# Gated networks with the first products by 2x2 blocks in seven block products, gated values through DRAM, second products by chunk

## The chip, the cores and the metric

One core of a Trainium2 chip runs the whole program. TensorE (PE) multiplies, VectorE (DVE), ScalarE (ACT) and GpSimd (POOL) do the rest, and SyncE (SP) issues most of the DMAs, each of its instructions in order. The metric is the device time of one execution in microseconds (us).

## The reference, cut to what matters

Two layers; each is a token mixer (layer 0: a state space model, S5, with a gated output; layer 1: attention with 8 heads) and a SwiGLU network. There are 1024 latent and 256 context tokens, 1024 features, and 2816 inner features.

```
def swiglu(h, w_in, w_out):
    gate, up = jnp.split(h @ w_in, 2, axis=-1)
    return (jax.nn.silu(gate) * up) @ w_out
...
    val, gate = jnp.split(z @ w_glu, 2, axis=-1)
    return (val * jax.nn.sigmoid(gate)) @ w_out, jnp.stack(finals, axis=1)
...
  x <- LayerNorm(alpha * x + gate * sublayer(x * (1 + scale) + shift)).
```

## The kernel before, in words

Activations lie feature-major: 8 k-tiles of 128 features by three chunks of tokens (CH): chunk 0 and chunk 1 with 512 latent tokens each, chunk 2 with the 256 of the context. They live in 88 "pages" (128 x 512 floats) and 13 half pages. Every product is made of three passes in fp32r: each operand is split into hi (ACT copies it, L95 and L124) and lo (DVE subtracts, L96 and L125), and `mm3` (L110) multiplies hi by hi (L114), hi by lo (L116) and lo by hi (L118), with n matmuls each for the chunks that it is given.

Weights are blocks of 128 x 1024, used in the order of `wseq`. `w_load` starts their loads on SP into two raw tiles (`wr`), `w_ahead` splits them by halves up to LS blocks ahead of the one that `w_next` hands out.

There are three gated networks: the mixer's output of layer 0 (8 tiles of 128 inner features, 8 outer ones) and two SwiGLU networks (22 tiles). In each, `glu_head` makes the first tile or two by chunk, `glu_body` (L717) the rest: for each inner tile one weight block of the gate and one of the value, each over all three chunks at once (`gemm_all`); `glu_gate` (L680) takes the activation on ACT (L685), multiplies by the value on DVE (L688) and splits the result. After every two inner tiles `out_all` multiplies them by their two blocks of the second weights, and DVE adds the scaled sums to the residual `acc` in SBUF (L655, `accumulate`). The last six tiles' second products are left for `tail_units`, by chunk, with their weights split once and kept.

`boundary` (L879) puts the end of a network, its layer norm and the next first products together: the products of chunk 0, then those of chunk 1 with the steps of chunk 0's norm between them, then those of chunk 2 with chunk 1's norm, then the next network's first tiles (heads) by chunk. An estimated clock and the list YW set after how many us of products the next step of a norm is emitted. The norm (`layer_norm`, L803) has matmuls of its own in PE's stream: the mean (L818), the mean square (L834), and the spread of the inverse root (L814), and on DVE the subtraction (L821), the sum of squares (L825, L829), the scaling (L844) and half of the affine maps (L849); POOL makes the lo of h (L852).

## Time and profile before

| | |
|---|---|
| median of 3 runs | 3405.5 us (3402.41 to 3406.01) |
| span of the profiled execution | 3407.8 us |
| PE busy | 3308.8 us, 18298 matmuls |
| DVE, ACT, POOL busy | 1781.3, 1071.3 and 368.6 us |
| bytes moved by DMA | 244.99 MB |

The profiled execution's own time is its span, from the first to the last instruction; the runs were timed apart from it, and their median is 2.3 us less than the span. A busy PE is not a PE at its peak: matmuls overlap, so that the pitch of their starts tells more than their durations. The rows further down name a line, an engine, an operation, the tile that it writes <- the tiles that it reads, shapes and counts.

### The profile page before, as it was taken

How to read it: one execution, taken by the hardware profiler on the slowest of the kernel's cores; microseconds unless marked ns; L12 is line 12 of the kernel's file. 1: busy time of each engine (PE TensorE's matmuls, PEld its weight loads, DVE VectorE, ACT ScalarE, POOL GpSimd, SP SyncE). 2: the span in 40 equal slices, each digit the busy share in tenths (PEclk: the TensorE clock that was granted, in tenths of full speed). 3: DMA queues.
4: the chain of work that ended last, by engine and by line, in shares of the span. 5: the costliest groups of instructions: out<-in, count | busy, mean ns of one | idle time of the engine just before them, and what ended most of it. 6: DMA issues, size and time to landing. Idle time of an engine off the chain costs nothing.

```text
span 3407.8 us, 45779 instructions
## 1 busy us (share of the span) xinstructions
PE 3308.8 (97%) x18298; PEld 2772.1 (81%) x18298; DVE 1781.3 (52%) x3883; ACT 1071.3 (31%) x2143; POOL 368.6 (11%) x387
## 2 busy tenths in 40 slices
PE   8999689999999999999999999999999999999997
PEld 5763678888888888888888899998888888888886
DVE  7789733246333333332476888887743333333226
ACT  3351441124211111111254577774431111111213
POOL 1230100015000000000153310000410000000002
PEclk9999899999999999999999999999999999999998
DMA  7679971110111111111112100003011111111111
GB/s 256 174 211 325 248 212 38 50 50 15 48 38 38 38 38 38 38 38 49 57 63 86 62 21 17 29 7 118 26 38 38 38 38 38 38 38 38 46 42 62
DMA packets 156372, 244.99 MB, mean 72 GB/s; under 512 B 46480, under 2 KB 86064, under 8 KB 155392
## 3 DMA queue, kind: packets, MB, share of 16 engines
q1 hardware_dynamic: 148672, 217.12, 20.5%
q0 software_dynamic: 7488, 24.96, 2.4%
q8 instruction: 143, 2.34, 0.3%
q14 instruction: 69, 0.57, 0.1%
HBM read 205.86 MB, written 36.18 MB: 71 GB/s over the span
## 4 chain that ended last, share of the span: by engine, by line
PE 88%; DVE 8%; DMA 1%; ACT 1%; issue 1%; POOL 1%; SPq 0%; DVEq 0%; ACTq 0%; POOLq 0%
PE ps L114 24%; PE ps L116 24%; PE ps L118 24%; PE ps L1179 3%; DVE sw L530 2%; PE ps L1200 1%; PE ps L1198 1%; PE ps L1199 1%; PE ps L1137 1%; PE ps L1138 1%; PE ps L1139 1%; DVE X L536 1%; DVE sw L534 1%; PE ps L596 1%; DMA G<-dPF 1%
## 5 line engine op out<-in xcount | busy, mean ns | idle before, releaser
L114 PE MATMUL ps<-pg,pg 128*128 128x512 f32 (+1 forms) x3888 | 1103.6, 369 | 7.2 <-ACT pg L124 3.3
L116 PE MATMUL ps<-pg,pg 128*128 128x512 f32 (+1 forms) x3888 | 1096.6, 367 | 1.3 <-POOL pg L852 1.0
L118 PE MATMUL ps<-pg,pg 128*128 128x512 f32 (+1 forms) x3888 | 1094.7, 367 | 0.2 <-DVE pg L96 0.2
L114 PEld LDWEIGHTS ps<-pg,pg 128*128 128x128 f32 x3888 | 658.7, 189 | 128.6 <-issue 5.4
L116 PEld LDWEIGHTS ps<-pg,pg 128*128 128x128 f32 x3888 | 658.5, 189 | 117.9 <-POOL pg L852 1.2
L118 PEld LDWEIGHTS ps<-pg,pg 128*128 128x128 f32 x3888 | 658.1, 189 | 115.8 <-DVE pg L96 0.5
L96 DVE TENSOR_TENSOR pg<-wr,pg 128x512 fp32r<-128x512 f32 x384 | 250.0, 696 | 515.9 <-ACT pg L95 511.3
L655 DVE SCALAR_TENSOR_TENSOR pg<-ps,mods,pg 128x512 f32<-128x512 f32 (+1 forms) x560 | 342.7, 660 | 258.5 <-PE ps L118 256.0
L124 ACT ACTIVATE pg<-pg 128x512 fp32r<-128x512 f32 x142 | 88.9, 631 | 1005.5 <-DVE pg L688 987.9
L688 DVE TENSOR_TENSOR pg<-pg,ps 128x512 f32<-128x512 f32 x104 | 71.1, 683 | 528.3 <-PE ps L118 528.3
L95 ACT ACTIVATE pg<-wr 128x512 fp32r<-128x512 f32 x384 | 221.1, 628 | 213.7 <-PE ps L116 79.5
L642 POOL TENSOR_TENSOR pg<-pg,pg 128x512 f32<-128x512 f32 x8 | 10.4, 1297 | 2073.2 <-DVE pg L655 2073.2
L685 ACT ACTIVATE pg<-ps 128x512 f32<-128x512 f32 x104 | 57.0, 595 | 379.3 <-PE ps L118 379.3
L125 DVE TENSOR_TENSOR pg<-ps,pg 128x512 fp32r<-128x512 f32 (+1 forms) x210 | 141.9, 676 | 54.5 <-ACT pg L124 49.0
L1159 ACT ACTIVATE pg<-ps,nb,rq 128x512 f32<-128x512 f32 x192 | 148.8, 776 | 5.8 <-DVE sm L1168 2.6
L125 DVE TENSOR_TENSOR pg<-pg,pg 128x512 fp32r<-128x512 f32 x142 | 100.9, 716 | 84.4 <-ACT pg L124 84.1
L124 ACT ACTIVATE pg<-ps 128x512 fp32r<-128x512 f32 (+1 forms) x210 | 123.3, 587 | 55.2 <-PE ps L1179 47.7
L114 PE MATMUL ps<-hp,pg 128*128 128x256 f32 x480 | 138.0, 287 | 0.0
L1144 DVE TENSOR_REDUCE mx<-ps 128x1 f32<-128x512 f32 (+1 forms) x208 | 136.9, 660 | 1.3 <-PE ps L1139 1.3
L116 PE MATMUL ps<-hp,pg 128*128 128x256 f32 x480 | 136.4, 284 | 0.0
L118 PE MATMUL ps<-hp,pg 128*128 128x256 f32 x480 | 136.4, 284 | 0.0
L167 PE MATMUL ps<-gw,sS 128*32 128x512 f32 x384 | 114.4, 618 | 8.2 <-DMA gw<-in_w_mod 7.8
(314 smaller groups left out, 3877.2 us busy)
## 6 DMA issues: line engine op xcount, KB each, us to landing
gw<-in_w_mod SPq DMA_DIRECT2D x192, 256.0 KB, 5.2
wr<-in_w_ffn_in SPq DMA_DIRECT2D x88, 512.0 KB, 3.6
wr<-in_w_ffn_out SPq DMA_DIRECT2D x48, 512.0 KB, 3.5
dT<-to POOLq DMA_DIRECT2D x16, 512.0 KB, 4.4
U<-dUL SPq DMA_DIRECT2D x16, 512.0 KB, 4.9
wr<-in_w_s_glu SPq DMA_DIRECT2D x16, 512.0 KB, 3.7
x<-in_x SPq DMA_DIRECT2D x8, 640.0 KB, 8.7
wr<-in_w_s_out SPq DMA_DIRECT2D x10, 512.0 KB, 3.5
```

The lines of the kernel that those rows point to most:

```text
L95: nc.scalar.activation(hi, x, AF.Copy)
L96: nc.vector.tensor_tensor(lo, x, hi.bitcast(F32), op=ALU.subtract)
L114: mm(ps[c], wh, rh[c], start=first, stop=False)
L116: mm(ps[c], wh, rl[c], start=False, stop=False)
L118: mm(ps[c], wl, rh[c], start=False, stop=last)
L124: self.nc.scalar.activation(hi, src, AF.Copy)
L125: self.nc.vector.tensor_tensor(lo, src, hi.bitcast(F32), op=ALU.subtract)
L167: nc.tensor.matmul(g[32 * q:32 * q + 32, :], self.sS[:, k, :], t[k], start=(k < 4), stop=(k >= 4), tile_position=(0, 32 * q))
L655: self.nc.vector.scalar_tensor_tensor(acc[f][c], ps, gate[:, f, cd:cd + 1], acc[f][c], op0=ALU.mult, op1=ALU.add)
L1144: v.tensor_reduce(mx[:, kc:kc + 1], ps, axis=AX.X, op=ALU.max)
L1159: nc.scalar.activation(p, u["bank"].pop((qt, kc)), AF.Exp, bias=nb[:, 0:1], scale=rq, accum_out=sm[:, kc:kc + 1])
L1179: nc.tensor.transpose(pt[:, a, 128 * qt:128 * qt + 128], u["p"][qt, kt // 4][:, 128 * (kt % 4):128 * (kt % 4) + 128], self.ident)
```

## The change

Of each gated network, the first products of an inner tile over the 1024 latent tokens are seen as a product of 2x2 blocks: the weights by gate (A11, A12) and value (A21, A22) and by the first and last four k-tiles, the activations by the same k halves and by chunk (B11 is the first k half of chunk 0, B21 the last one, B22 the last k half of chunk 1). Seven block products with the sums S1 to S4 of weights and T1 to T4 of activations give what eight did. `ffn_pair` does one inner tile in nine steps (seven block products of 12 matmuls over 512 tokens, and two of 24 over the 256 context tokens); `i_step` makes the sums and splits of the weights, AHEAD = 4 items before they are used. The head tiles keep the plain form, and `x_sums` makes T1 to T4 beneath them.

The gated values go to DRAM (`spill`, tensor dI), and the second products are made afterwards, chunk by chunk over the whole depth (`out_chunks`): for each of 8 output features and each block of 8 k-tiles one weight block, loaded and split again for each chunk (`out_plan`), and the values read back and split once for each chunk (`z_ahead`). The residual goes to DRAM and comes back too (`keep`, `residual`). The attention's output product takes the same form. A third raw weight tile is added (`w_raw`), and the second weights are laid out by output feature.

```
+    def w_raw(self):
+        self.nr += 1
+        p = self.wpools[-(self.nr % 3 == 0 and len(self.wpools) == 2)]
+        return p.tile([P, 1024], F32, tag="wr", bufs=2 - (p is not self.wpools[0]), name=self.nm("wr"))
...
-            r = self.wpool.tile([P, 1024], F32, tag="wr", bufs=2, name=self.nm("wr"))
-            self.nc.sync.dma_start(r, self.wseq[self.wld])
+            r = self.w_raw()
+            n = self.wseq[self.wld].shape[1]
+            self.nc.sync.dma_start(r[:, :n], self.wseq[self.wld])
             self.wraw[self.wld] = r
...
+    def ffn_head(self, hh, hl, head, act, raw):
+        ls, self.LS = self.LS, 0
+        ws = [self.w_next() for _ in range(2 * head)]
+        self.LS = ls
+        s = {}
+        sums = []
+        def unit(t, half, c):
+            n = CH[c][1]
+            if c == 1 and t == half == 0:
+                self.x_start(hh, hl, raw)
+                sums.append(self.x_sums())
+                self.i_load()
+            ps = self.gemm(ws[2 * t + half], hh, hl, c)
+            if half == 0:
+                s[t, c] = self.pgn(n)
+                self.nc.scalar.activation(s[t, c], ps, act)
+            else:
+                x = s.pop((t, c))
+                self.nc.vector.tensor_tensor(x, x, ps, op=ALU.mult)
+                self.spill(t, c, x)
+            if sums:
+                for _ in range(16 // (4 * head)):
+                    next(sums[0], None)
+            if c == 2:
+                self.XC = [(hh[k][2], hl[k][2]) for k in range(KT)]
+                self.i_until(2 * t + half + 2)
+            return n / 100
+        return [[lambda t=t, h=h, c=c: unit(t, h, c) for t in range(head) for h in range(2)] for c in range(3)]
...
                 nc.gpsimd.tensor_tensor(hl[kt][c], t, hh[kt][c].bitcast(F32), op=ALU.subtract)
+                if raw is not None and c < 2:
+                    raw[kt][c] = t
...
+PROD = (("A11", "B11"), ("S1", "T1"), ("S2", "T2"), ("A12", "B21"), ("S3", "T3"), None, ("A22", "T4"), ("S4", "B22"), None)
+ITEMS = ("A11", "S1", "S2", "A12", "S3", "A22", "S4", "A21")
+NEED = (1, 2, 3, 4, 5, 5, 6, 7, 8)
+AHEAD = 4
...
+    def x_sums(self):
+        v, r = self.nc.vector, self.xr
+        for n in ("T1", "T2", "T3", "T4"):
+            for k in range(4):
+                t = self.page()
+                if n == "T1":
+                    v.tensor_tensor(t, r[k][1], r[k][0], op=ALU.subtract)
+                elif n == "T2":
+                    v.tensor_tensor(t, r[k + 4][1], self.xt["T1", k], op=ALU.subtract)
+                elif n == "T3":
+                    v.tensor_tensor(t, r[k + 4][1], r[k][1], op=ALU.subtract)
+                else:
+                    v.tensor_tensor(t, r[k + 4][0], self.xt["T2", k], op=ALU.subtract)
+                self.xt[n, k] = t
+                hi, lo = self.page(F32R), self.page(F32R)
+                self.nc.scalar.activation(hi, t, AF.Copy)
+                self.nc.gpsimd.tensor_tensor(lo, t, hi.bitcast(F32), op=ALU.subtract)
+                self.X[n].append((hi, lo))
+                yield
+        self.xr = self.xt = None
+    def i_load(self):
+        if self.il < len(self.pairs):
+            r = []
+            for h in range(2):
+                x = self.w_raw()
+                self.nc.sync.dma_start(x, self.win[2 * self.pairs[self.il] + h])
+                r.append(x)
+            self.iraw[self.il] = r
+            self.il += 1
+    def i_step(self):
+        nc = self.nc
+        v = nc.vector
+        n = 8 * len(self.pairs)
+        a, b, c = self.ik, self.ik - 1, self.ik - 2
+        self.ik += 1
+        if a < n:
+            i, name = a // 8, ITEMS[a % 8]
+            while self.il <= i:
+                self.i_load()
+            g, u = self.iraw[i]
+            A = {"A11": g[:, :512], "A12": g[:, 512:], "A21": u[:, :512], "A22": u[:, 512:]}
+            if name[0] == "A":
+                t = A[name]
+            else:
+                t = self.page()
+                x, y, op = {"S1": ("A21", "A22", ALU.add), "S2": ("S1", "A11", ALU.subtract),
+                            "S3": ("A11", "A21", ALU.subtract), "S4": ("A12", "S2", ALU.subtract)}[name]
+                x, y = (A[z] if z in A else self.isum[i, z] for z in (x, y))
+                v.tensor_tensor(t, x, y, op=op)
+            self.isum[i, name] = t
+        if 0 <= b < n:
+            i, name = b // 8, ITEMS[b % 8]
+            hi = self.ihi[i, name] = self.page(F32R)
+            nc.scalar.activation(hi, self.isum[i, name], AF.Copy)
+        if 0 <= c < n:
+            i, name = c // 8, ITEMS[c % 8]
+            hi, lo = self.ihi.pop((i, name)), self.page(F32R)
+            v.tensor_tensor(lo, self.isum[i, name], hi.bitcast(F32), op=ALU.subtract)
+            self.isp[i, name] = (hi, lo)
+            if name == "A21":
+                self.iraw.pop(i)
+                for z in ITEMS:
+                    self.isum.pop((i, z))
+                if self.il < i + 3:
+                    self.i_load()
+    def i_until(self, k):
+        while self.ik - 2 < min(k, 8 * len(self.pairs)):
+            self.i_step()
+    def spill(self, t, c, x):
+        o, n = CH[c]
+        self.nc.sync.dma_start(self.dI[t][:, o:o + n], x)
+    def ffn_last(self, s):
+        if s >= 4:
+            self.w_ahead(0.5 * (s - 3))
+    def ffn_pair(self, i, act, last=None):
+        nc = self.nc
+        v, mm = nc.vector, nc.tensor.matmul
+        t = self.pairs[i]
+        W = {}
+        e = {}
+        def product(ps, a, b, first, stop):
+            wh, wl = W[a]
+            for k in range(4):
+                xh, xl = self.X[b][k]
+                o = slice(P * k, P * k + P)
+                for j, (p, q) in enumerate(((wh, xh), (wh, xl), (wl, xh))):
+                    mm(ps, p[:, o], q, start=(first and k == 0 and j == 0), stop=(k == 3 and j == 2), skip_group_check=True)
+        def ctx(a, b):
+            ps = self.psum()[:, :256]
+            for k in range(KT):
+                wh, wl = W[(a, b)[k // 4]]
+                o = slice(P * (k % 4), P * (k % 4) + P)
+                xh, xl = self.XC[k]
+                for j, (p, q) in enumerate(((wh, xh), (wh, xl), (wl, xh))):
+                    mm(ps, p[:, o], q, start=(k == 0 and j == 0), stop=(k == KT - 1 and j == 2))
+            return ps
+        for s in range(9):
+            self.i_until(8 * i + NEED[s] + AHEAD)
+            if last:
+                last(s)
+            for z in ITEMS[:NEED[s]]:
+                if z not in W:
+                    W[z] = self.isp.pop((i, z))
+            if s == 0:
+                R = self.psum()
+                product(R, *PROD[s], True, True)
+                s1 = self.page()
+                nc.scalar.activation(s1, R, AF.Copy)
+            elif s == 1:
+                Q = self.psum()
+                product(Q, *PROD[s], True, True)
+            elif s == 2:
+                product(R, *PROD[s], False, True)
+                s2 = self.page()
+                nc.scalar.activation(s2, R, AF.Copy)
+            elif s == 3:
+                B = self.psum()
+                product(B, *PROD[s], True, True)
+                v.tensor_tensor(s1, s1, B, op=ALU.add)
+                nc.scalar.activation(s1, s1, act)
+            elif s == 4:
+                product(R, *PROD[s], False, True)
+                t22 = self.page()
+                v.tensor_copy(t22, Q)
+                v.tensor_tensor(t22, t22, R, op=ALU.add)
+            elif s == 5:
+                ps = ctx("A11", "A12")
+                g = self.half()
+                nc.scalar.activation(g, ps, act)
+            elif s == 6:
+                product(R, *PROD[s], False, True)
+                v.tensor_tensor(s1, s1, R, op=ALU.mult)
+                self.spill(t, 0, s1)
+            elif s == 7:
+                product(Q, *PROD[s], False, True)
+                v.tensor_tensor(s2, s2, Q, op=ALU.add)
+                nc.scalar.activation(s2, s2, act)
+                v.tensor_tensor(s2, s2, t22, op=ALU.mult)
+                self.spill(t, 1, s2)
+            else:
+                ps = ctx("A21", "A22")
+                v.tensor_tensor(g, g, ps, op=ALU.mult)
+                self.spill(t, 2, g)
+    def out_plan(self, wout, nk):
+        return [w[:, o:min(o + 1024, P * nk)] for _ in range(3) for w in wout for o in range(0, P * nk, 1024)]
+    def spilled(self, c, i):
+        o, n = CH[c]
+        z = self.pgn(n)
+        self.nc.sync.dma_start(z, self.dI[i][:, o:o + n])
+        return z
+    def residual(self, x, f, c):
+        o, n = CH[c]
+        self.nc.sync.dma_start(x, self.dX[f][:, o:o + n])
+    def z_ahead(self, k, load=None):
+        nk = self.znk
+        while self.zl < min(3 * nk, k + (ZL if load is None else load)):
+            self.zr[self.zl] = self.zraw(self.zl // nk, self.zl % nk)
+            self.zl += 1
+        while self.zk < min(3 * nk, k):
+            c = self.zk // nk
+            if c < 2:
+                hi, lo = self.page(F32R), self.page(F32R)
+            else:
+                p = self.page(F32R, (P, 2, 256))
+                hi, lo = p[:, 0, :], p[:, 1, :]
+            self.split(hi, lo, self.zr.pop(self.zk))
+            self.zs[c, self.zk % nk] = hi, lo
+            self.zk += 1
+    def out_chunks(self, acc, gate, residual):
+        v, g = self.nc.vector, self.nc.gpsimd
+        nk = self.znk
+        st = {}
+        def unit(c, f, lo):
+            o, n = CH[c]
+            hi = min(lo + 8, nk)
+            if lo == 0:
+                st["ps"] = self.psum()[:, :n]
+                acc[f][c] = self.pgn(n)
+                residual(acc[f][c], f, c)
+            w = self.w_next()
+            for i in range(lo, hi):
+                if f == 0:
+                    self.z_ahead(nk * c + i + 1 + ZS)
+                x, y = self.zs[c, i]
+                self.mm3([st["ps"]], *(z(P * (i - lo)) for z in w), [x], [y], i == 0, i == nk - 1)
+                if f == 7:
+                    self.zs.pop((c, i))
+                    if c < 2 and i >= 2:
+                        self.z_ahead(nk * (c + 1) + min(i - 1, ZE))
+            if hi == nk:
+                self.accumulate(acc, gate, f, c, st["ps"])
+                if f == 1:
+                    rs = self.rs[c] = self.pgn(n)
+                    g.tensor_tensor(rs, acc[0][c], acc[1][c], op=ALU.add)
+                if f > 1:
+                    (v if f == 7 else g).tensor_tensor(self.rs[c], self.rs[c], acc[f][c], op=ALU.add)
+            return 3 * (hi - lo) * n / 2220
+        return [[lambda c=c, f=f, o=o: unit(c, f, o) for f in range(8) for o in range(0, nk, 8)] for c in range(3)]
...
+ZL, ZS, ZE = 3, 2, 12
...
+        def keep(kt, c):
+            o, n = CH[c]
+            nc.sync.dma_start(self.dX[kt][:, o:o + n], acc[kt][c])
+        def body(act, nk, raw):
+            n = len(self.pairs)
+            for i in range(n):
+                self.ffn_pair(i, act, self.ffn_last if i == n - 1 else None)
+            self.X = self.XC = None
+            self.LS = 1.5
+            self.out_start(nk, raw)
...
+        def ffn(l, cols, outs, acc):
+            win = L("w_ffn_in", l)
+            self.wseq += win[:4]
+            self.i_start(win, range(2, NF))
+            raw = [[None] * 2 for _ in range(KT)]
+            self.cross(outs, acc, cols, lambda hh, hl: self.ffn_head(hh, hl, 2, AF.Silu, raw), keep, raw)
+            self.wseq += self.out_plan(L("w_ffn_out", l), NF)
+            body(AF.Silu, NF, self.spilled)
+            acc = new()
+            return self.out_chunks(acc, self.mod(l, 5), self.residual), acc
...
-        self.glu_body(zh, zl, *S5P, AF.Sigmoid, acc, self.mod(0, 2))
+        self.wseq += self.out_plan(L("w_s5_out"), KT)
         zh = zl = None
-        outs = self.glu_tail(8, 2, 4, acc, self.mod(0, 2))
...
+        body(AF.Sigmoid, KT, self.spilled)
...
-        self.wseq += self.glu_weights(L("w_ffn_in", 0), L("w_ffn_out", 0), *FFP)
-        hh, hl = self.cross(outs, acc, self.ln_cols(0, 0, 0, 3, 4), lambda hh, hl: self.glu_head(hh, hl, 2, AF.Silu))
-        self.glu_body(hh, hl, *FFP, AF.Silu, acc, self.mod(0, 5))
-        hh = hl = None
-        outs = self.glu_tail(NF, 2, 4, acc, self.mod(0, 5))
...
+        outs, acc = ffn(0, self.ln_cols(0, 0, 0, 3, 4), outs, acc)
...
+        self.wseq += self.out_plan(L("w_o"), KT)
+        self.LS = 1.5
+        self.out_start(KT, lambda c, h: self.ao[h][c])
+        ahead = {(k // 2, 2 * (k % 2)): [lambda k=k: self.w_ahead(0.5 * k + 0.5)] for k in range(3)}
+        ahead.update({(2 + k // 3, 2 * (k % 3)): [lambda k=k: self.z_ahead(k + 1, 0)] for k in range(6)})
+        ahead[4, 0] = [lambda: self.z_ahead(8, 0)]
...
-        self.out_all(ws.__getitem__, tl[0:2], acc, g, each=lambda: some(2))
-        ws = [self.w_next(), self.w_next()]
-        for i, j in enumerate((1, 3, 4, 6)):
-            todo.insert(j, lambda i=i: self.w_ahead(0.5 * i + 0.5))
-        self.out_all(ws.__getitem__, tl[2:4], acc, g, (0,), each=lambda: some(1))
-        some(len(todo))
-        self.LS = 2
-        self.ao = None
-        outs = self.tail_units(tl[4:] + tl[2:4], 4, acc, g)
...
+        outs = self.out_chunks(acc, self.mod(1, 2), self.residual)
+        outs, acc = ffn(1, self.ln_cols(1, 0, 1, 3, 4), outs, acc)
```

## Rows read from the trace of the kernel before

**Rows 1.** Span and mean granted clock of the core.

```profile
core 0: 3407.8 us, clock 0.984
```

**Rows 2.** The page's busy times: us, share, instructions of each engine.

```profile
PE 3308.8 (97%) x18298; PEld 2772.1 (81%) x18298; DVE 1781.3 (52%) x3883; ACT 1071.3 (31%) x2143; POOL 368.6 (11%) x387
```

**Rows 3.** The chain that ended last, shares by engine.

```profile
PE 88%; DVE 8%; DMA 1%; ACT 1%; issue 1%; POOL 1%; SPq 0%; DVEq 0%; ACTq 0%; POOLq 0%
```

**Rows 4.** Stretches: length, busy us (instructions) by engine, clock, DMA share, GB/s.

```profile
820.00:1680.00 860.00, 860.00 (x4398) 730.64 (x4397) 293.63 (x517) 151.88 (x289) 24.95 (x27) 1.00 0.13 41
740.00:820.00 80.00, 76.04 (x408) 65.17 (x407) 61.90 (x116) 33.77 (x53) 34.17 (x29) 0.98 0.09 27
1680.00:1760.00 80.00, 76.98 (x452) 67.12 (x451) 63.55 (x117) 34.02 (x52) 35.10 (x30) 0.98 0.14 47
2390.00:2460.00 70.00, 66.39 (x360) 57.54 (x359) 51.03 (x99) 29.14 (x43) 28.10 (x24) 0.95 0.08 26
3330.00:3408.00 78.00, 55.30 (x314) 47.96 (x312) 53.97 (x125) 27.34 (x45) 14.32 (x15) 0.84 0.19 68
```

**Rows 5.** Timeline of PE, three stretches: start, us, operation.

```profile
900.37 0.75 PE L116 MATMUL ps<-pg,pg 128*128 128x512 f32 x3
...
902.13 0.75 PE L116 MATMUL ps<-pg,pg 128*128 128x512 f32 x3
...
766.10 0.39 PE L118 MATMUL ps<-pg,pg 128*128 128x512 f32 x1
...
777.69 0.39 PE L118 MATMUL ps<-pg,pg 128*128 128x512 f32 x1
...
784.72 0.28 PE L118 MATMUL ps<-hp,pg 128*128 128x256 f32 x1
...
796.95 0.28 PE L118 MATMUL ps<-hp,pg 128*128 128x256 f32 x1
```

**Rows 6.** Groups by line and shape: count | busy us, mean ns | idle before.

```profile
L655 DVE SCALAR_TENSOR_TENSOR pg<-ps,mods,pg 128x512 f32<-128x512 f32 x384 | 272.0, 745 | 251.1 <-PE ps L118 248.6 <-DMA pg<-dX 2.3
L96 DVE TENSOR_TENSOR pg<-wr,pg 128x512 fp32r<-128x512 f32 x384 | 250.0, 696 | 515.9 <-ACT pg L95 511.3
L95 ACT ACTIVATE pg<-wr 128x512 fp32r<-128x512 f32 x384 | 221.1, 628 | 213.7 <-PE ps L116 79.5 <-DMA wr<-in_w_ffn_in 70.8 <-DMA wr<-in_w_o 30.5
L688 DVE TENSOR_TENSOR pg<-pg,ps 128x512 f32<-128x512 f32 x104 | 71.1, 683 | 528.3 <-PE ps L118 528.3
L852 POOL TENSOR_TENSOR pg<-pg,pg 128x512 fp32r<-128x512 f32 x48 | 64.6, 1378 | 50.1 <-ACT pg L851 50.1
L685 ACT ACTIVATE pg<-ps 128x512 f32<-128x512 f32 x104 | 57.0, 595 | 379.3 <-PE ps L118 379.3
L825 DVE TENSOR_TENSOR pg<-pg,pg 128x512 f32<-128x512 f32 x40 | 34.3, 857 | 0.0
L688 DVE TENSOR_TENSOR hp<-hp,ps 128x256 f32<-128x256 f32 x52 | 21.6, 415 | 7.0 <-PE ps L118 7.0
```

**Rows 7.** Timeline of DVE in a norm: start, us, operation.

```profile
1688.88 0.67 DVE L821 TENSOR_TENSOR pg<-pg,ps 128x512 f32<-128x512 f32 x1
1689.48 0.68 DVE L825 TENSOR_TENSOR pg<-pg,pg 128x512 f32<-128x512 f32 x1
```

**Rows 8.** DMA issues: count, KB each, median us from issue to landing.

```profile
wr<-in_w_ffn_in SPq DMA_DIRECT2D x88, 512.0 KB, 3.6
...
pg<-dQ SPq DMA_DIRECT2D x16, 256.0 KB, 2.8
```

**Rows 9.** Timeline of SP's queue: reload of the residual (14 of 256 KB, 7 of 128 KB).

```profile
2310.11 14.28 SPq L1386 DMA_DIRECT2D pg<-dX  x21
```

**Rows 10.** Timeline of PE about a stop in a norm.

```profile
758.05 1.06 PE L834 MATMUL ps<-ones,pg 128*128 128x1 f32 x8 [2.80 <-DVE pg L829]
...
759.55 0.63 PE L116 MATMUL ps<-pg,pg 128*128 128x512 f32 x1
759.97 0.63 PE L118 MATMUL ps<-pg,pg 128*128 128x512 f32 x1
```

**Rows 11.** What PE waited for: us in total, times, longest.

```profile
PE ps L834 <- DVE pg L829: 10.2, 4, 2.8
PE ps L834 <- DVE hp L829: 8.4, 2, 7.0
```

**Rows 12.** The chain that ended last, its end: start, us, what.

```profile
3382.90 0.49 DVE pg L655
...
3400.42 2.99 ACT pg L872 x5
```

More of the change, by code (lines that the diff above doesn't have):

```diff
@@ L800, in rsqrt, with layer_norm @@
             v.scalar_tensor_tensor(out if it == 2 else y, t, 1.5, y, op0=ALU.add, op1=ALU.mult)
-    def layer_norm(self, acc, c, cols, hh, hl, ready, after=None):
+    def layer_norm(self, acc, c, cols, hh, hl, ready, after=None, raw=None):
         nc = self.nc
@@ L1303, in run @@
             self.rest()
-            self.wpool.release()
+            for p in self.wpools[::-1]:
+                p.release()
             self.pages.release()
@@ L1313, in rest @@
         L = self.rows
-        S5P, FFP = self.S5P, (NF, 2, 2, 4)
+        new = lambda: [[None] * 3 for _ in range(KT)]
+        def keep(kt, c):
[18 more added lines that the diff above has]
+            return self.out_chunks(acc, self.mod(l, 5), self.residual), acc
+        self.wpools.append(tc.alloc_tile_pool(name="w2", bufs=1, side="left", reuse_waits="tile"))
         self.LS = 2
-        zh, zl = self.fm(F32R), self.fm(F32R)
-        zz = {}
+        zh, zl, zz = self.fm(F32R), self.fm(F32R), new()
         def zload(c):
@@ L1337, in rest @@
         zload(1)
-        heads = self.glu_head(zh, zl, 1, AF.Sigmoid)
+        self.i_start(L("w_s5_glu"), range(1, 8))
+        heads = self.ffn_head(zh, zl, 1, AF.Sigmoid, zz)
         zsplit(8)
@@ L1373, in rest @@
         hh = hl = None
-        wo = L("w_o")
-        self.wseq += wo + wo[2:4]
-        acc, tl = [[None] * 3 for _ in range(KT)], []
-        def reload(kts):
-            for kt in kts:
-                for c, (o, n) in enumerate(CH):
-                    if c < 2:
-                        acc[kt][c] = self.page()
-                    elif kt % 2 == 0:
-                        p = self.page(F32, (P, 2, 256))
-                        acc[kt][2], acc[kt + 1][2] = p[:, 0, :], p[:, 1, :]
-                    nc.sync.dma_start(acc[kt][c], self.dX[kt][:, o:o + n])
@@ L1388, in split @@
-        def split(h, c):
-            if c == 0 and len(tl) == h:
-                tl.append((self.pages2(F32R), self.pages2(F32R)))
-            self.split(tl[h][0][c], tl[h][1][c], self.ao[h][c])
-        ahead = {(k // 2, 2 * (k % 2)): [lambda k=k: self.w_ahead(0.5 * k + 0.5)] for k in range(4)}
-        ahead.update({(2 + k // 3, 2 * (k % 3)): [lambda k=k: split(k // 3, k % 3)] for k in range(6)})
-        ahead[4, 0] = [lambda: reload([0])]
+        self.wseq += self.out_plan(L("w_o"), KT)
```

78 lines of the change are left out of this document (36 added, 42 removed).

## The prediction

> **What bounds the kernel now.** I read the core's span and clock first, 3407.8 us at 0.984 of full speed [rows 1], then the busy times: PE is busy for 97% of the span, DVE for half [rows 2]. The chain that ended last puts 88% on PE and 8% on DVE [rows 3]. The stretches say where: in the body of a SwiGLU network PE has not a nanosecond of idle time, 4398 matmuls in 860 us; in the boundaries between networks it idles 4.0, 3.0 and 3.6 us, and in the last 78 us 22.7 us [rows 4]. So there matters, first, how many matmuls there are and at what pitch they start, and second, what stops PE at the boundaries.
>
> The pitch is read from the timeline, not from durations. In the body, where two 512-column matmuls and one of 256 alternate, three take (902.13 - 900.37) / 3 = 0.587 us; 860 us / 1466 triples gives the same [rows 4, 5]. By chunk, 51 starts of 512 columns take 11.59 us, 0.227 each, and 102 of 256 columns 12.23 us, 0.120 each [rows 5]. A triple by chunk is thus 0.574 us: alternating costs 0.013.
>
> **PE's part of the change.** A pair (inner tile) before: 16 x 3 x 2 = 96 matmuls of 512 for the latents. Now seven products of 12 = 84, so 12 x 0.227 = 2.72 us less. There are 20 + 20 + 7 = 47 such pairs: 128 us. The count of second products does not change, but all are now by chunk. A SwiGLU network has 66 x 24 = 1584 triples, of which heads (96) and tail (144, chunk 0's partly) were by chunk already; 1344 lose 0.013 us, 17.9 us. The mixer's network has 384 such triples (5.1 us), the attention's output 48 (0.6). Sum: 128 + 2 x 17.9 + 5.1 + 0.6 = **169 us less on PE**. A pair then takes 84 x 0.227 + 48 x 0.120 = 24.8 us.
>
> **Is a pair still PE's?** DVE has 4 sums, 8 lo parts, 6 evacuations of 512 and one of 256: 12 x 0.696 + 6 x 0.683 + 0.415 = 12.9 us; ACT 8 x 0.628 + 4 x 0.595 + 0.4 = 7.8 us [rows 6]. Both lie under 24.8. PSUM bank R is read by ACT after steps 0 and 2 and by DVE after 4 while PE does another product of 2.7 us; the copy takes 0.6. I cost the pair's evacuations, spills and sums at nothing; the cover is 12 us of idle DVE in each pair. The raw tiles are three, and a pair takes two: the value block of the next pair waits on SP for this pair's gate block, with the last pair's spills queued behind it. The gate block is last read by S4's sum, about 1.3 us into the pair; the load lands 3.6 us later [rows 8]; DVE needs it for the next S1 before it adds the result of step 3, which PE ends at 10.9 us. Some 5 us are left. Removed with the body are most of the additions to `acc` (384 at 0.745 us [rows 6]); DVE hid them, so they bring nothing.
>
> **Start of the second products.** The first z read is behind the last pair's last spill on SP: 0.4 us for DVE's product, 2.8 us for 256 KB to land, 0.6 for ACT's hi and 0.7 for lo [rows 6, 8], 4.5 us in which PE has nothing. For its first feature PE takes 22 x 0.68 = 15 us, but 22 reads of 256 KB, two weight blocks and the residual are 7.1 MB. The reload of the residual issued 4.6 MB in 14.28 us, 0.32 MB/us [rows 9]: 22 us, 7 more. So 11.5 us for each SwiGLU network, 8 for the mixer's (8 values: 9 us of reads over 5.4 of PE), nothing for the attention, whose values are in SBUF and split beneath the last head: **31 us**. The bounds: 0 if reads came ahead (the queue's order excludes it), or 4.5 + 46 per network if they came one at a time.
>
> The Trainium skill ("DMA: Bandwidth & Descriptors", sections Bandwidth and Anatomy of one DMA) wants DMAs of 1 MiB or more and gives a single one 2.0 us plus bytes at 436 GB/s, 2.6 us for 256 KB. By that, alone in the queue, 22 reads would be 57 us instead of the 22 that the row gives. Its figure is for the software path; the row shows SP's reads 0.68 us apart, so I go by the row.
>
> **Norms against weights.** Before, six blocks were split once and kept while chunks 1 and 2 ran. Now each chunk splits all blocks again, on the same DVE that runs the norm. A chunk's norm has on DVE some 8 subtractions, 7 sums, 8 scalings and 4 maps of 0.68 to 0.86 us, and 13 small ones: 20 to 23 us. DVE's starts in a norm are 0.60 us apart [rows 7], so I count 0.6 per operation. From the norm's first step to its mean-square matmul PE gets 11 us of products. In chunk 2 of a SwiGLU network, DVE must meanwhile do 9.4 us of norm, ten splits of weights (6), ten of values (4) and some additions: 21 us, where 14 have passed. PE, in order, stops there 7 us; with 8 tiles 4 us. In chunk 1, with 15 us of products for a feature, 5 and 1. Four boundaries: 2 x (7 + 5) + 2 x (4 + 1) = **34 us**. The bounds: 0, and twice as much if DVE is at its means instead of its pitch and POOL's additions hold it up. Before, this same wait cost 18.6 us in all [rows 11].
>
> **Heads and ramps.** T1 to T4 add 16 sums on DVE, 16 copies on ACT and 16 subtractions of 1.38 us on POOL [rows 6], 22 us under 33 us of products; DVE also starts the first pair's items. I take 2 us for each of three heads, **6 us**. After a stop of 2.8 us PE's starts were 0.42 us apart instead of 0.227, for about seven matmuls [rows 10], 1.4 us; for some six more stops **8 us**.
>
> **Given back.** The idle time of the three boundaries, 10.6 us, and their ramps, some 4, are counted anew above; and at the end chunk 1's norm no longer runs into the tail. From the last addition to the last scalings pass 20 us [rows 12], of which I take 5 off: together **20 us**.
>
> **Sum.** 3407.8 - 169 + 31 + 34 + 6 + 8 - 20 = 3298; the median of the runs is 2.3 us below the profiled span, so 3295 us.
>
> **The rivals.**
>
> A: the transitions cost little, because DVE and ACT run ahead of PE and their queues are filled beneath the slow first features. For it: DVE is busy for only half of the span [rows 2]. Then PE's 169 and the 20 remain, with three starts of 4.5: 3407.8 - 169 - 20 + 14 - 2 = 3230 us.
>
> B: the transitions cost double (79 more). For it: in the boundaries DVE is busy for 61.9 of 80 us even before [rows 4], and sums that run beside POOL take 0.857 us instead of 0.683 [rows 6]. 3374 us, still faster.
>
> C, slower: a pair is starved of pages. T1 to T4, B and the context take 64 of the 88 pages; at step 4 seven split items (14), a hi part, two sums, three evacuations and two spills are alive, 86. If spills come late on SP, ACT's copies wait for a page of a product that PE has just ended, and the four items of lead are gone; each item then costs 0.6 + 0.6 + 0.7 us on the path. It decides from 110 / 47 = 2.3 us for a pair; two late items, 4 us, make it 3295 + 188 = 3483 us. Against it: a page freed one product earlier still leaves two products, 5 us.
>
> D, slower: the reads do not overlap. Each of 22 then takes its 2.8 us [rows 8]: 62 us over 15 in chunk 0, 62 over 30 (last and first features) in chunk 1, about 55 over 23 in chunk 2, in two networks 220 us: some 3500. The 0.68 us between reads [rows 9] speaks against it. [...]
>
> E: the change does not do what it says: reuse of bank R stops PE at steps 2, 4 and 6 by nearly a microsecond each, 2.7 us for a pair. Nothing of the gain from seven products remains: 3295 + 128 = 3423 us, about the time before.
>
> **How the numbers follow.** Forecast 0.45 (its own range 3255 to 3335), A 0.18, B 0.22, C 0.10, D 0.03, E 0.02. The range takes the forecast, nearly all of A and most of B: 3228 to 3375. About 0.2% is what a measurement of this kernel can tell from no change: faster 0.84 (forecast, A, B without its end), same 0.03 (that end and E), slower 0.13 (C, D).
>
> **What would show it.** In the pairs' stretch: no idle PE, 132 matmuls in 24.8 us. At each start of second products 4 to 5 us of idle PE that end with an ACT or DVE split of a value. The largest waits on DVE at the mean-square matmul of chunk 1's norm, beneath chunk 2. Wrong it would be by idle PE inside pairs (C, E), by reads that land at intervals of over 1 us (D), or by out-stage features that take longer than 22 x 0.68 us right through, which would mean that splitting, not PE, sets the second products.

## The result, and the profile after

The changed kernel takes 3428.0 us (median; 3423.2 to 3435.4) beside 3405.8 for the kernel before: a ratio of 1.0066, 95% interval 1.005 to 1.0082. It is 0.66% slower, where 3.2% faster was forecast. The span and clock of its profile, and the page's busy times:

```profile
core 0: 3424.8 us, clock 0.965
```

```profile
PE 3199.5 (93%) x17734; PEld 2693.8 (79%) x17734; DVE 2109.5 (62%) x4279; ACT 1384.6 (40%) x2721; POOL 463.6 (14%) x435
```

Beside [rows 1, 2]: PE has 564 = 47 x 12 matmuls fewer, but is busy only 109 us less, and its idle time (span less busy) has grown from 99 to 225 us. A third number is in the clock: the trace notes the stretches in which TensorE was granted 0.50. Half of PE's busy time in them is lost: 31.4 us before, 77.8 after (part of each stretch falls on idle time, where it costs nothing). Work at full clock is then 3308.8 - 31.4 = 3277.4 us before and 3199.5 - 77.8 = 3121.7 after: **156 us less**, where the prediction had 169. The same sum gives 3117 to 3123 us for every other kernel below with these 17734 matmuls, so it holds to some 3 us. **Idle time took back 126, the clock 46**: -155.7 + 126.3 + 46.4 is the 17 us by which the span grew.

Where they were lost, stretch by stretch (length, busy us and instructions of PE, PEld, DVE, ACT, POOL, clock, DMA share, GB/s): the pairs, the second products in their middle, the four transitions, the counterpart of the second of [rows 4], and the last 78 us.

```profile
1000.00:1050.00 50.00, 50.00 (x267) 43.30 (x266) 24.05 (x39) 14.02 (x26) 0.00 (x0) 1.00 0.22 69
1450.00:1500.00 50.00, 50.00 (x222) 41.44 (x221) 15.57 (x21) 12.04 (x22) 4.82 (x3) 1.00 0.30 104
...
668.00:896.00 228.00, 189.99 (x911) 159.21 (x910) 149.75 (x253) 107.27 (x193) 73.61 (x64) 0.90 0.40 137
1397.00:1770.00 373.00, 333.86 (x1651) 282.74 (x1649) 197.36 (x338) 143.95 (x261) 53.40 (x42) 0.94 0.50 165
2385.00:2563.00 178.00, 151.12 (x759) 128.00 (x758) 128.64 (x219) 81.05 (x144) 70.15 (x59) 0.91 0.33 110
3063.00:3425.00 362.00, 323.84 (x1630) 276.27 (x1630) 189.35 (x341) 133.16 (x250) 26.64 (x21) 0.95 0.49 162
...
740.00:820.00 80.00, 58.06 (x289) 48.83 (x287) 49.52 (x86) 36.37 (x67) 23.32 (x21) 0.83 0.39 128
...
3347.00:3425.00 78.00, 58.03 (x455) 56.61 (x454) 44.16 (x103) 30.04 (x56) 7.66 (x9) 0.88 0.47 149
```

The pairs are as forecast: 267 matmuls in 50 us is 132 in 24.7 us, with no idle time. So are the second products once they run: 222 in 50 us, 0.225 each. Most of the loss lies in the four stretches from the last pair of a network (for the third, from the attention) to the next pairs, heads or the end: 142 us idle in 1141 us, at clocks of 0.90 to 0.95, where the kernel before idles for 33 us at the same places. About the first norm, 740 to 820 us, PE idles for 22 us at 0.83, where before it was 4 us at 0.98.

What PE waited for (us in total, times, longest), the answer to [rows 11], and one row of the same view for SP's queue:

```profile
PE ps L121 <- ACT pg L131: 65.1, 16, 9.8
PE ps L121 <- ACT pg L102: 32.3, 12, 7.1
...
PE ps L853 <- DVE rstd L839: 15.1, 5, 5.7
...
PE ps L873 <- DVE hp L868: 9.3, 2, 6.0
PE ps L1079 <- ACT pg L1102: 8.6, 3, 4.4
...
PE ps L873 <- DVE pg L868: 4.1, 2, 2.3
```

```profile
SPq L1621 <- ACT pg L913: 135.8, 14, 22.2
```

The prediction looked for the largest waits on DVE at the norm's mean square (now L873). These are 13.4 us, less than the 18.6 before. The largest are on ACT: splits of values (L131) and of weights (L102). The SP row leads to a cause: the store of the normed residual (L1621, `keep`) stands on SP until ACT has made its value (L913), 135.8 us in 14 waits. One such ring, on SP, ACT and PE (start, us, operation, in brackets the idle time before and what ended it):

```profile
751.68 0.33 SPq L87 DMA_DIRECT2D wr<-in_w_s_out  x1
770.68 2.26 SPq L1621 DMA_DIRECT2D dX<-pg  x2
773.02 0.38 SPq L1682 DMA_DIRECT2D pg<-in_x  x1
773.50 0.40 SPq L87 DMA_DIRECT2D wr<-in_w_s_out  x1
...
769.85 0.80 ACT L913 ACTIVATE pg<-pg,ba,ga 128x512 f32<-128x512 f32 x1
775.93 0.63 ACT L1683 ACTIVATE pg<-pg 128x512 f32<-128x512 f32 x1 [5.28 <-DMA pg<-in_x]
776.47 1.13 ACT L102 ACTIVATE pg<-wr 128x512 fp32r<-128x512 f32 x2
...
769.62 0.39 PE L125 MATMUL ps<-pg,pg 128*128 128x512 f32 x1
777.13 0.80 PE L121 MATMUL ps<-pg,pg 128*128 128x512 f32 x1 [7.12 <-ACT pg L102]
777.72 0.63 PE L123 MATMUL ps<-pg,pg 128*128 128x512 f32 x1
778.15 0.63 PE L125 MATMUL ps<-pg,pg 128*128 128x512 f32 x1
```

SP issues nothing from 752.0 to 770.7, because its next entry is a store that needs the norm's last step (L913, done at 770.65). Behind it stand the residual and the next weights. ACT, in order too, waits 5.28 us for that residual (L1683), with the split of weights (L102) behind that, and PE stops for 7.12 us. Then it goes on at a start every 0.43 us instead of 0.227. The Trainium skill ("TensorE: Matmul & The Clock Gate", section Architectural detail: the array is 16× 32×32, not 1× 128×128) calls ACT's queue strictly first in, first out; the trace agrees: the split follows the scaling with no wait of its own.

The starts of the second products, as PE, SP and ACT show the first:

```profile
665.37 3.03 PE L1088 MATMUL ps<-pg,pg 128*128 128x256 f32 x24
675.47 0.79 PE L121 MATMUL ps<-pg,pg 128*128 128x512 f32 x1 [7.07 <-ACT pg L131]
...
669.73 8.12 SPq L1148 DMA_DIRECT2D pg<-dI  x13
...
674.12 0.63 ACT L1683 ACTIVATE pg<-pg 128x512 f32<-128x512 f32 x1 [6.68 <-DMA pg<-in_x]
```

PE stops for 7.07 us here, 9.80 and 6.27 in the SwiGLU networks. The 13 reads are issued 0.62 us apart, close to the 0.68 of [rows 9]; they overlap.

### The profile page after: what moved, and what is told of

Same layout as the page of the kernel before. It is cut to its first block, busy times and chain, and to the rows that moved or that the text cites. A ratio compares the mean times of both kernels' runs of the same rounds, so it can differ in the third digit from the quotient of the medians.

```text
span 3424.8 us, 47261 instructions
## 1 busy us (share of the span) xinstructions
PE 3199.5 (93%) x17734; PEld 2693.8 (79%) x17734; DVE 2109.5 (62%) x4279; ACT 1384.6 (40%) x2721; POOL 463.6 (14%) x435
## 4 chain that ended last, share of the span: by engine, by line
PE 74%; DVE 5%; ACT 2%; DMA 2%; issue 1%; POOL 1%; SPq 0%; ACTq 0%; DVEq 0%; POOLq 0%
PE ps L1079 26%; PE ps L123 9%; PE ps L121 9%; PE ps L125 9%; PE ps L1088 8%; PE ps L1478 3%; PE ps L1499 1%; PE ps L1497 1%; PE ps L1498 1%; PE ps L1436 1%; PE ps L1437 1%; PE ps L1438 1%; DVE pg L103 1%; ACT pg L102 1%; DMA pg<-dI 1%
## 5 line engine op out<-in xcount | busy, mean ns | idle before, releaser
L1079 PE MATMUL ps<-pg,pg 128*128 128x512 f32 x3948 | 919.3, 391 | 13.8 <-ACT pg L1102 8.6
L1079 PEld LDWEIGHTS ps<-pg,pg 128*128 128x128 f32 x3948 | 738.8, 189 | 165.5 <-ACT pg L1102 9.9
L121 PE MATMUL ps<-pg,pg 128*128 128x512 f32 (+1 forms) x2112 | 740.6, 370 | 103.1 <-ACT pg L131 65.1
L123 PE MATMUL ps<-pg,pg 128*128 128x512 f32 (+1 forms) x2112 | 731.7, 366 | 7.2 <-DVE pg L132 4.3
L125 PE MATMUL ps<-pg,pg 128*128 128x512 f32 (+1 forms) x2112 | 726.9, 364 | 6.0 <-DVE pg L103 5.9
L121 PEld LDWEIGHTS ps<-pg,pg 128*128 128x128 f32 x2112 | 407.8, 197 | 176.6 <-ACT pg L131 69.6
L123 PEld LDWEIGHTS ps<-pg,pg 128*128 128x128 f32 x2112 | 406.6, 197 | 76.1 <-DVE pg L132 11.9
L125 PEld LDWEIGHTS ps<-pg,pg 128*128 128x128 f32 x2112 | 406.9, 197 | 67.5 <-DVE pg L103 10.4
L103 DVE TENSOR_TENSOR pg<-wr,pg 128x512 fp32r<-128x512 f32 (+1 forms) x444 | 331.0, 788 | 182.2 <-ACT pg L102 178.2
L102 ACT ACTIVATE pg<-wr 128x512 fp32r<-128x512 f32 (+1 forms) x444 | 244.8, 597 | 325.4 <-DMA wr<-in_w_ffn_out 230.1
L1088 PEld LDWEIGHTS ps<-pg,pg 128*128 128x128 f32 x2256 | 283.1, 191 | 7.3
L1088 PE MATMUL ps<-pg,pg 128*128 128x256 f32 x2256 | 285.3, 283 | 0.0
L662 DVE SCALAR_TENSOR_TENSOR pg<-ps,mods,pg 128x512 f32<-128x512 f32 x64 | 47.9, 749 | 233.6 <-PE ps L125 226.3
L1044 DVE TENSOR_TENSOR pg<-pg,pg 128x512 fp32r<-128x512 f32 x188 | 137.8, 733 | 77.4 <-ACT pg L1040 77.4
L131 ACT ACTIVATE pg<-ps 128x512 fp32r<-128x512 f32 (+1 forms) x210 | 124.0, 590 | 70.8 <-PE ps L1478 47.6
L1127 DVE TENSOR_TENSOR pg<-pg,ps 128x512 f32<-128x512 f32 x47 | 32.3, 688 | 193.1 <-PE ps L1079 193.1
L1113 DVE TENSOR_TENSOR pg<-pg,ps 128x512 f32<-128x512 f32 x47 | 32.3, 688 | 191.2 <-PE ps L1079 191.2
L1044 DVE TENSOR_TENSOR pg<-wr,pg 128x512 fp32r<-128x512 f32 x188 | 133.4, 709 | 2.2 <-ACT pg L1040 2.2
```

The lines of the kernel that those rows point to most:

```text
L102: nc.scalar.activation(hi, x, AF.Copy)
L103: nc.vector.tensor_tensor(lo, x, hi.bitcast(F32), op=ALU.subtract)
L121: mm(ps[c], wh, rh[c], start=first, stop=False)
L123: mm(ps[c], wh, rl[c], start=False, stop=False)
L125: mm(ps[c], wl, rh[c], start=False, stop=last)
L131: self.nc.scalar.activation(hi, src, AF.Copy)
```

## The experiments

Two theories stood at first. **ORDER**: SP's order makes weights and residual late. **DVE**: the splits made again in each chunk, on the engine that runs the norm, are too much work; this is the mechanism of the prediction's step on norms. Medians in us, against the runs of the kernel before beside them (its medians were 3406.3, 3406.6 and 3407.9); idle PE and clock from each profile (the profiled executions of "values early", "lead of 20" and "eight products" took 9, 8 and 6 us more than the median):

| kernel | time | ratio to before (95%) | idle | clock |
|---|---|---|---|---|
| changed | 3428.0 | 1.0066 (1.005 to 1.0082) | 225 | 0.965 |
| stores off SP | 3396.2 | 0.9967 (0.9955 to 0.9979) | 206 | 0.970 |
| values early | 3398.6 | 0.9978 (0.9964 to 0.9992) | 205 | 0.963 |
| lead of 20 | 3405.8 | 1.0002 (0.9992 to 1.0011) | 217 | 0.966 |
| these three | 3361.0 | 0.9867 (0.985 to 0.9883) | 178 | 0.972 |
| eight products | 3543.1 | 1.0403 (1.0388 to 1.0419) | 215 | 0.964 |
| three, lead of 3 blocks | 3364.3 | 0.9878 (0.9863 to 0.9893) | 178 | 0.970 |
| three, norm spread | 3365.3 | 0.9887 (0.9872 to 0.9902) | 186 | 0.973 |
| three, both and no scaling | 3369.0 | 0.9894 (0.9877 to 0.991) | 187 | 0.972 |
| changed, no lo parts | 3382.1 | 0.9932 (0.9916 to 0.9949) | 196 | 0.970 |
| three, no lo parts | 3305.7 | 0.9705 (0.969 to 0.972) | 142 | 0.979 |
| three, heads | 3347.1 | 0.9824 (0.9809 to 0.9839) | 166 | 0.976 |
| three, heads, reuse | 3338.6 | 0.9803 (0.9786 to 0.982) | 157 | 0.975 |

**Stores off SP.**

```
         def keep(kt, c):
             o, n = CH[c]
-            nc.sync.dma_start(self.dX[kt][:, o:o + n], acc[kt][c])
+            (nc.gpsimd if kt % 2 else nc.scalar).dma_start(self.dX[kt][:, o:o + n], acc[kt][c])
```

> One edit to the changed kernel: the 24 stores of the residual at each of three boundaries are issued by the engine that makes the value (ACT for even tiles, POOL for odd ones) and not by SP, so that no load on SP stands behind a store that waits for the norm's last step. Theory ORDER (most of the loss in the transitions is SP's order: weights and residual stand behind stores that wait): 3428 falls by 45 to 60 us, to 3370 to 3383; the stops of PE that end with a split of weights on ACT, 32 us now, fall below 12 us, and PE's idle time below 190 us. Theory DVE (the loss is the work that norm and splits put on DVE, as the prediction's step Norms against weights had it; SP's waits follow from it): within 6 us of 3428, the stops move from ACT's splits to DVE's. Loss through the edit: 36 issues each on ACT and POOL at up to 0.6 us could cost up to 10 us.

32 us less: by far more than DVE allowed, short of ORDER. PE's waits in this kernel, and its stop in the ring above:

```profile
PE ps L121 <- ACT pg L131: 48.8, 14, 10.1
...
PE ps L121 <- ACT pg L102: 21.0, 8, 5.8
```

```profile
776.65 0.50 PE L121 MATMUL ps<-pg,pg 128*128 128x512 f32 x1 [2.33 <-ACT pg L102]
```

That stop is 2.33 us long instead of 7.12. Waits for weights fell from 32.3 to 21.0 us, not below 12, and idle time to 206, not below 190. So SP's order is a cause, and not the only one. The Trainium skill ("DMA: Bandwidth & Descriptors", section Issuing engines are not separate DMA queues) says that issuing from several engines saves only the sequencer's time to issue, usually small. Here 72 issues moved were worth 32 us: not for their own time, but because the queue behind a store that waits was free.

**Values early.** `out_start` goes ahead of the pairs, and `ffn_last` reads and splits the first gated values in the last pair.

```
+            self.out_start(nk, raw)
...
     def ffn_last(self, s):
         if s >= 4:
             self.w_ahead(0.5 * (s - 3))
+        if s >= 2:
+            m = self.znk - 1
+            k = min(m, max(0, 2 * s - 7))
+            self.z_ahead(k, min(m, 2 * s) - k)
```

> One edit to the changed kernel: reads of the first gated values are issued and split during the last pair of each network, instead of after it, as far as the values of the pairs before have been written. Theory START (the stops of 7.07, 9.80 and 6.27 us before the first second product and the wait of the residual behind them come only from the order): 25 to 30 us less than 3428, 3398 to 3403, and of each of those stops under 2 us is left. Rival PACE (the reads and splits are as slow as they are, an early start only moves the stop into the first feature): at most 10 us less, 3418 to 3428, with stops of 1 to 5 us spread over the first feature.

29 us less, as START had it, though of the three stops (7.07, 9.80 and 6.27 us) 4.0, 2.2 and under 0.8 us are left.

**Lead of 20.** `ZL, ZS, ZE = 3, 2, 12` becomes `3, 2, 20`.

> One number changed in the changed kernel: in the last feature of a chunk up to 20 values of the next chunk are split ahead instead of 12. Theory NORM BEHIND (the stops in the first features of chunks 1 and 2, 21 us in sum, are value splits that stand on ACT and DVE behind the norm's steps; done earlier they are gone): 12 to 20 us less than 3428, 3408 to 3416. Rival MOVED (DVE and ACT are the limit of that stretch, the splits then delay the last feature): within 5 us of 3428.

22 us less, a little above its range: the value splits in the first features stood behind the norm's steps, and there was time for them earlier.

**These three together.**

> The three edits of the other kernels of this call together. ORDER with START and NORM BEHIND: 80 to 110 us less than 3428, 3318 to 3348, below the kernel before (3405). DVE with PACE and MOVED: 3410 to 3430, no better than one of them alone. If the sum of the three single gains is larger than this gain by over 15 us, the same stops were counted twice.

67 us less than the changed kernel and 1.3% below the kernel before, short of the 80 to 110 that the three theories had together. The single gains sum to 83: some 16 us of stops were counted twice.

**Eight products.** How much the seven products are worth by themselves:

```
                 Q = self.psum()
                 product(Q, *PROD[s], True, True)
+                product(Q, *PROD[s], True, True)
```

> The changed kernel, but in each of the 47 pairs the product of step 1 is computed twice, so that a pair has eight block products (96 matmuls of 512) again; nothing else differs. Theory PE PAIR (a pair is PE's, as the prediction had it, and one product fewer is worth 47 x 12 x 0.227 us): 128 us more than 3428, 3550 to 3562. Rival (DVE, spills or pages set the pair's time, and seven products bring less): 3428 to 3520, with idle PE in the pairs of the changed kernel.

```profile
PE 3332.0 (94%) x18298; PEld 2802.5 (79%) x18298; DVE 2109.5 (59%) x4279; ACT 1384.3 (39%) x2721; POOL 465.0 (13%) x435
```

115 us more by the medians, just short of PE PAIR's range and above its rival's, and 122 by the spans. Work at full clock, by the sum above, is 3332.0 - 82.4 = 3249.6 us: 128 more, the very price. Idle time is down by 10 us, since in the longer pairs the first ones wait less for ACT and DVE (7.1 us where the changed kernel has 13.8); the clock takes 5 more. The work was saved, and the loss is elsewhere.

**Lead of 3 blocks, norm spread, both.** On the kernel with the three edits, what remained were stops of 5 to 6 us. ACT before one of them:

```profile
1642.36 0.63 ACT L862 ACTIVATE pg<-pg 128x512 f32<-128x512 f32 x1 [1.50 <-DVE pg L860]
1643.55 0.63 ACT L862 ACTIVATE pg<-pg 128x512 f32<-128x512 f32 x1 [0.57 <-DVE pg L860]
1644.75 0.63 ACT L862 ACTIVATE pg<-pg 128x512 f32<-128x512 f32 x1 [0.57 <-DVE pg L860]
1645.29 1.13 ACT L102 ACTIVATE pg<-wr 128x512 fp32r<-128x512 f32 x2
1646.33 0.71 ACT L131 ACTIVATE pg<-hp 128x256 fp32r<-128x256 f32 x2
```

ACT's squares (L862) wait for DVE's subtractions of the norm one by one, and the split that PE needs (L131) is last. A longer lead or smaller batches should help, if batches are what is wrong.

```
-            self.LS = 1.5
+            self.LS = 3
```

> The kernel with the three edits (3361 us), and in the second products of the three gated networks weights are split up to 3 blocks ahead instead of 1.5. Theory LEAD (the stops that remain there come because a batch of norm operations, 6 to 9 us on ACT, stands ahead of the next block's split, and the lead of 1.5 blocks of 5.4 us is as long as that; DVE's and ACT's whole work is not the limit): stops on a split of weights fall from 19.5 to below 8 us, and the time by 12 to 30 us, as PE's clock recovers too: 3331 to 3349. Theory DVE/ACT LIMIT (the two engines can't do more in these stretches, a lead is used up): within 6 us of 3361.

```
+        Y = list(YW)
+        if c == 0:
+            Y[1], Y[5], Y[6] = 5.4, 5.4, 5.4
+        if c == 1:
+            Y[5] = 2.7
...
+            self.alt = not self.alt
+            i = int(self.alt and len(gens) > 1 and ready[gens[0][0]])
+            t = next(gens[i][1], None)
```

> The kernel with the three edits, and the norm's steps are spread: for chunk 0 each step (two tiles) waits for one more block of products, for chunk 1 half as much, and the last steps of chunk 1's norm alternate with the first of chunk 2's. The work is the same. Theory LUMPS (not the amount of work but its batches make ACT and DVE late): stops on splits of weights and values in chunks 1 and 2 fall by half, from 42 to about 20 us, and the 5.8 us before the heads of chunk 2 shorten: 3335 to 3350. Theory DVE/ACT LIMIT: within 6 us of 3361.

```
-            nc.scalar.activation(x, x, AF.Copy, scale=ALPHA)
-        outs = self.out_chunks(acc, self.mod(0, 2), scaled)
+        gs = self.cp.tile([P, KT, 2], F32, name="gs0")
+        nc.vector.tensor_scalar(gs, self.mod(0, 2), 1.0 / ALPHA, None, op0=ALU.mult)
+        self.eps = EPS / ALPHA ** 2
+        outs = self.out_chunks(acc, gs, scaled)
```

> The kernel with the three edits, the lead of 3 blocks and the spread norm together; besides, in the mixer's network the residual is not scaled on ACT, its factor is taken into the gate and the norm's epsilon, so that ACT does not wait there for the residual's transfer. LEAD and LUMPS together: 3310 to 3335, idle PE below 130 us; the third edit alone some 3 to 8 us of it. DVE/ACT LIMIT: 3350 to 3361.

All three miss: 3, 4 and 8 us more. With the longer lead the waits for weights fell to 13.9 us, not below 8, and with the norm spread to 7.1 (from 19.5), but those for values rose from 22.5 to 29.6 and 31.7: the stops moved. LEAD and LUMPS fall. The first two times lie within the 6 us of DVE/ACT LIMIT, the third outside the ranges of both.

**No lo parts.** The work itself is taken away (`nolo` holds the weight blocks of the second products), on the changed kernel and on the one with the three edits. Both kernels leave the lo parts of these weights out of their results and serve the question only:

```
-            nc.vector.tensor_tensor(lo, x, hi.bitcast(F32), op=ALU.subtract)
+            if self.wls not in self.nolo:
+                nc.vector.tensor_tensor(lo, x, hi.bitcast(F32), op=ALU.subtract)
...
-                self.mm3([st["ps"]], *(z(P * (i - lo)) for z in w), [x], [y], i == 0, i == nk - 1)
+                wz = w[0](P * (i - lo))
+                self.mm3([st["ps"]], wz, wz, [x], [y], i == 0, i == nk - 1)
```

> The changed kernel, but the lo parts of the second products' weights are not computed (384 subtractions of up to 512 columns on DVE, some 240 us of its time, left out); the third matmul of each triple uses the hi part instead, so that PE's work is the same and the second products are less exact. Theory DVE (splitting the weights again in each chunk, on the DVE that runs the norm, is what makes the transitions slow): 60 to 100 us less than 3428, 3328 to 3368, with the waits for ACT gone as well, since ACT waits for DVE's norm. Theory ORDER (SP's order makes weights and residual late, DVE has time enough): 10 to 35 us less, 3393 to 3418, and the waits on ACT's splits of weights and values stay above 60 of their 97 us.

> The kernel with the three edits (3361 us), again without the 384 subtractions. If DVE's work is what is left there: 25 to 45 us less, 3316 to 3336. If what is left are single waits of the heads and of first features: within 12 us of 3361.

The first is 46 us less, between the two theories, and 82 of the 97 us of waits on ACT's splits stay, as ORDER had it; the second 55 us less than the kernel with the three edits, above what DVE's work was expected to be worth. From the changed kernel the three edits bring 67 and this one 46, both together 122, a little over the sum: two causes that add up. What PE waits for in the second:

```profile
PE ps L123 <- ACT pg L133: 15.9, 6, 3.4
...
PE ps L123 <- ACT pg L103: 8.4, 6, 3.0
```

Its waits for splits of values and weights are 24 us instead of 97, its clock 0.979.

**Heads, reuse.** Two changes of order (`n2` counts the steps of chunk 2's norm, of which the fourth is its inverse root), then one that does less work by keeping a chunk's last split blocks for the next chunk:

```
+                if f == 7 and c < 2:
+                    self.z_ahead(nk * (c + 1) + nk, 0)
...
+            if c == 1 and hd[c]:
+                run(hd[c][:-1])
+                while self.n2 < 4:
+                    clock[1] = clock[0] + step()
+                run(hd[c][-1:])
```

> The kernel with the three edits, and two more in the order of issue: all values of the next chunk are split before the next chunk begins (20 of 22 now), and before the last product of the heads of chunk 1 the norm of chunk 2 is taken on to its inverse root, so that a product of 5.4 us runs beside it. Theory SINGLE WAITS: the stops of 5.8 us before the heads of chunk 2 (twice) and those of some 5 us in the first features of chunk 2 (twice) shrink to under 2 us, with the clock 15 to 28 us less than 3361: 3333 to 3346. Theory DVE LIMIT: the stops move to the next wait, within 8 us of 3361.

```
+ORD = list(range(8)), list(range(7, -1, -1)), list(range(8))
...
+            f = ORD[c][p]
...
+            if c and p == 0:
+                w = st.pop(("w", j))
```

> As the kernel with the changed heads, and every second chunk goes through the features in the other order, so that the last feature's split weights serve the next chunk's first too: 6 of 72 blocks in a SwiGLU network, 2 of 24 in the two others, are loaded and split once less, just when the norm's statistics run. Theory DVE: 16 blocks by two splits of 0.6 us, 20 us of DVE's time less where it is short: 10 to 25 us less than without it, 3315 to 3335. Theory SINGLE WAITS: within 5 us of the kernel with the changed heads.

14 us less for the first, just short of its range: the late inverse root (5.8 us, twice) has become a wait for the mean square (5.4, twice), and the gain is that of the first features, where the two stops of 5 us are gone. Another 8.5 us for the second, below the 10 to 25 of theory DVE and above the 5 of SINGLE WAITS; the runs of the two kernels overlap (3343 to 3353 and 3336 to 3348), so this step is not clear of noise. At 3338.6 us, 2.0% below the kernel before, this is the fastest complete kernel:

```profile
core 0: 3333.7 us, clock 0.975
```

## Why the prediction was wrong

**PE's part** was right but for 13 us: 156 us by the sum above for 169. The test with eight products shows the 128 of the seven products whole; the rest, 41 us for second products by chunk in the prediction, is then 28, and no run shows why. **Is a pair still PE's?** Yes, 24.7 us and no idle time; the 12 us of idle DVE covered it. With that rivals C and E fall; E's wait, PE at bank R until ACT has copied it (L1102), shows only in the first pair of each of the three networks, 8.6 us in all.

**Start of the second products**, 31 us: the sum fits by luck (29 us came back when the reads went ahead). The three stops, 23.1 us with some 7 of lower clock behind them, stood for 13.5 of stops and 17.5 of slow features. The stops were longer than 4.5 us, since reads stand behind SP's last spill, weights and residual, and in the mixer the first split stands behind the residual's scaling; the features after it lost less. Rival D falls: reads come 0.62 us apart. The Trainium skill's price of one DMA ("DMA: Bandwidth & Descriptors", section Anatomy of one DMA), 2.6 us by its figures as the prediction has it, is for one alone; no run here issues them so.

**Norms against weights** is the step that failed, in size and by what it left out. It took the one wait that the trace before showed, DVE at the mean square, and priced the new splits as a delay there, 34 us (its 7 us for chunk 2 set 21 against 14, where it had just given PE 11, and it does not say why). That wait did not grow at all: 13.4 us for 18.6. The step asked of DVE's queue what stands behind what, and not of SP's and ACT's. The runs show three things in its place. DVE's subtractions alone are worth 46 to 55 us. The stores, which the prediction did not cost at all, hold up loads on SP, 32 us. Value splits behind the norm cost 22 us. The last two overlap with each other and with the start, 67 us for the three edits. These are waits of engines that work in order on rings across SP, ACT, DVE and PE, and no engine is at its limit over the whole stretch: DVE is busy for 665 of 1141 us there.

**Heads and ramps**: 6 us for heads stood for the 13.8 us that PE waits in first pairs and for two waits of 5.7 us for the inverse root before the heads of chunk 2, which no term had. 8 us for ramps stood for 46, since it counted six stops at 1.4 us; the price held, the count did not. The stretches (columns as above) right after five stops, of 7.12, 4.45, 3.33, 9.80 and 2.53 us:

```profile
777.10:781.20 4.10, 4.07 (x10) 3.16 (x11) 1.96 (x3) 1.20 (x2) 1.98 (x2) 0.50 0.17 65
787.20:790.60 3.40, 3.13 (x12) 2.71 (x12) 3.16 (x7) 1.59 (x4) 0.00 (x0) 0.50 0.29 107
794.10:798.20 4.10, 3.84 (x16) 3.55 (x17) 1.61 (x4) 0.97 (x2) 0.00 (x0) 0.50 0.56 168
1407.10:1412.70 5.60, 5.51 (x12) 4.08 (x13) 5.54 (x9) 5.17 (x10) 0.00 (x0) 0.50 1.05 388
1550.10:1556.00 5.90, 5.49 (x23) 4.29 (x24) 5.46 (x11) 2.78 (x6) 0.00 (x0) 1.00 0.31 90
```

After the first four PE works at the lower of its two levels (1.2 and 2.4 GHz, granted 0.50) for 3.4 to 5.6 us, so these stops cost 1.7 to 2.8 us more than their length; after the fifth the clock stayed up. From 440 us on, stops of over 1 us number 12 before and 43 after: 46 us on 31 more stops are 1.5 each. Between the changed kernel and the three edits without lo parts, idle time falls by 84 us and what the clock takes by 34 (77.8 to 44.3). That the clock follows the stops is read from such rows; no run changed the clock alone.

**Given back**: of the 5 us at the end 2.7 came (20.0 us idle in the last 78, for 22.7).

Net of what was given back the forecast's transitions cost 31 + 34 + 6 + 8 - 20 = 59 us; they cost 126 + 46 = 172. With the three edits and without the lo parts 43 + 13 = 56 us are left, no more than the forecast allowed, so the causes named make up the miss. Rival B, with 79 more (138 us), had the direction and too small a factor; it scaled the wait already seen, and no rival asked what a store that waits holds up. One thing stays open: how DVE's 46 to 55 us divide into its own time, ACT's waiting for it and the lo part for which PE's third matmul no longer waits, since no run separated these.

## What to carry to other kernels

A store of a value that is made late, put on the queue that also brings the next loads, turns into a stop of PE: for every DMA that a change adds, ask what its queue holds behind it until its source is ready, and let the engine that makes the value issue it. Where a change trades PE's work for passes through DRAM and repeated splits, the gain in the middle is easy to count (156 us here) and most of the loss lies in the transitions; add up each engine's work and order there, count the stops, and price each with the lower clock that follows it (here 1.5 us on average). A longer lead and smaller batches only moved the stops here; less work on DVE helped (46 to 55 us), and so did two changes of order (14 us), where the trace credits the values that were split before their chunk begins.

## What was not expected of the hardware

What the clock cost did not follow the length of the stop in proportion: after one of 3.33 us PE ran 4.1 us at a granted 0.50, after one of 9.80 us 5.6, and after one of 2.53 us not at all. And 72 DMAs issued from ACT and POOL beside their own work cost less than they brought: POOL was busy 0.59 us with each of its 36, the 21 us by which its busy time rose (463.6 to 484.5); each of ACT's took 0.33 us, which the busy time (1384.6 to 1385.8) does not count.
